# A two-layer decoder trunk on one core: gate paths first, values in six groups, masked compression, an opening in units of one and two k-tiles

## The chip, the core and the metric

The kernel runs on one core of one Trainium2 chip. The metric is the device time of one execution in microseconds, as the median of several runs. Engines are named as in the profile: PE (matrix products), PEld (its weight loads), DVE (VectorE), ACT (ScalarE), POOL (GpSimd), SP (the engine whose queue issues nearly all DMA requests).

## The reference

The input is x, 256 tokens of 1024 features in f32, and a conditioning vector c of 1024. Two layers, each `x = x + gate * mixer(rms_norm(x) * (1 + scale) + shift)`, where shift, scale and gate are three parts of `silu(c) @ w_ada + b_ada` (1024 by 3072 for each layer), and a last rms_norm.

The even mixer projects the 256 normalised tokens to 2968 columns and splits them:

- A: eight query heads of 64, one key and one value head, with rope, a sliding window of 128, and a learned sink for each head in the softmax.
- B: eight query heads in two groups, three branches: compressed keys and values (blocks of 32 with stride 16, through a small MLP with two weight matrices of 2048 by 256), selected blocks, and a window of 512. With 256 tokens all blocks are selected, so the second and third branch are causal attention. A sigmoid gate for each head and branch weighs the three.
- za and zb, 512 columns each: the outputs of A and B are multiplied by their silu before one output projection of 1024 by 1024.

The odd mixer projects to q, k, v, z of 1024 each, with 16 heads; with 256 tokens it is causal attention. Its output is multiplied by silu(z) and goes through an output projection of 1024 by 1024.

## The kernel before, in words

**Products.** A projection splits both operands into a rounded part and a rest (`split`: `whi` by ACT, `wlo` by DVE, in pieces of 512 columns) and makes three products for each k-tile (`mm3`: hi by hi, hi by lo, lo by hi). `hhi` and `hlo` hold the normalised input of a layer in that form, 128 features by 256 tokens for each of eight k-tiles; `ghi` and `glo` hold the gated attention output. Scores, transposes, values and small sums are plain f32 products.

**Order.** No engine instruction is issued where the code stands. `Plan.record` (line 229) notes each with what it depends on, and `Plan.issue` (line 259) issues all in the order of a list of numbers, ORDER (line 36), which was written out ahead. So each engine's own order is that list's, and all DMA requests of SP stand in one queue in that order. A request into a buffer waits in that queue until the buffer is free, with all requests behind it. As every instruction is issued from line 256, the profile shows L256 for nearly all, and tiles tell them apart. Buffers come from small rings (`rot`, line 300): five `raw` tiles of 128x2048 for weights, four `t4` of 128x1024, five `sm` and four `pT` for softmax, and eight banks of PSUM in rings ("pj" three, "s" two, "pt", "o" and "m" one each).

**Opening** (lines 647 to 735). c is transposed and its silu goes into `cz`. x is transposed as it is into `xT`; its root mean squares are spread over partitions by a product with ones (`rb`). Then a loop over eight k-tiles g. `start_prep` loads 256 columns of w_ada for k-tile g (128 of shift, 128 of scale; four requests of 256 KB, one k-tile ahead), sums them over 1024 rows, on DVE for `v` in `ST_ON`, on PE for `p`, makes `hhi[g]` and `hlo[g]` (h by DVE, `hhi` from h by ACT, `hlo` by DVE), and loads row block g of W0 in four requests. `start_mm` makes the products of 1688 columns: the queries, keys and values of B, the keys and values of A, the branch gates, and the first half of A's queries. The other half follows as a projection of its own (`ld_qa`, line 749).

**First layer** (lines 737 to 1036). Rope and transposes; `attn_pair` for two heads and one branch: scores, mask and minimum (DVE), exp (ACT), reciprocal and normalisation (DVE, `sm<-sm,rc`), transposes (PE), copies (ACT, `pT`), values (PE). `b_pair` calls it for two branches of two heads, `a_pair` for two heads, `compress` and `cmp_softmax` make the compressed branch, `cmp_pair` adds its output to `oT` with DVE, `fin_o` copies an output to `oT` with ACT, and `gated` (line 970) makes the products of a gate path, takes tanh, and multiplies with `oT`. `fill` puts jobs between them that sum w_ada for this layer's gate and the next layer's shift and scale (`acc`). Then `out_proj`, in which `add_scaled` adds to x.

**Second layer** (lines 1039 to 1221). Normalisation and transposes, then four times: values, queries and keys of four heads (`split_quad`, `rot_quad`), `attn_quad`, which ends with an ACT copy of 128x512 to `oT`. The four gate paths come behind all attention in the program. The output projection, the last normalisation and the store end it.

Of the kernel before, what the change touches and what calls it, by code (L numbers as in the profile page):

```python
# [7 lines left out]
F32 = mybir.dt.float32  # L8
# [5 lines left out]
P = 128  # L14
# [8 lines left out]
ST_ON = "ppvvpvvp"  # L23
AHEAD = 1
# [4 lines left out]
CUT = 384  # L29
T4B = 4  # L30
# [151 lines left out]
class Plan:  # L182
# [46 lines left out]
    def record(self, eng, name, args, kw):  # L229
# [11 lines left out]
        for a in banks:  # L241
            p0, p1, _ = self._box(a)
            uses.append((a.tensor.name + "#", (p0, p1, 1), eng.key == "pe" and not accum))
# [1049 lines left out]
```

## Time and profile before

| | |
|---|---|
| median of 3 runs | 318.71 us (318.41 to 320.02) |
| profiled execution | 317.62 us |
| its span in the profile | 315.8 us |
| mean granted clock of PE | 0.99 |
| DMA | 71.85 MB, mean 227 GB/s |

The span is the time from the first to the last instruction that the profile shows; 1.8 us of the profiled execution lie around it. A row of a group gives the engine, the operation, the tiles written and read, the shape and the count, then busy us and mean ns of one, then idle time ahead of them. Instructions of one engine overlap a little, so counts times means come out somewhat above busy time. An f32 product shows as two instructions on PE. A busy PE isn't a PE at its peak: ends of products are modelled.

### The profile page before, as it was taken

To read this page: it belongs to the slowest core of one execution; us is meant where nothing else is said; L and a number is where in the kernel's file an instruction comes from. 1 tells how busy PE (TensorE), PEld (TensorE's weight loads), DVE (VectorE), ACT (ScalarE), POOL (GpSimd) and SP (SyncE) were. 2 spreads that over 40 slices of the span, in tenths; PEclk is the share of its full clock that TensorE was granted. 3 is DMA by queue.
4 is the path that set the end of the run, shared out by engine and by line. 5 is a ranking of instruction groups with operands and counts; after the bars stand their busy time and mean duration, and the time that the engine had idled before them with its cause. 6 is when DMAs were issued, how large, how long until landed. Compare 5 with 4: busy or idle time off the path is not lost.

```text
span 315.8 us, 6311 instructions
## 1 busy us (share of the span) xinstructions
PE 300.0 (95%) x2246; PEld 251.0 (79%) x2246; DVE 271.1 (86%) x744; ACT 189.9 (60%) x481; POOL 12.3 (4%) x30
## 2 busy tenths in 40 slices
PE   6788999999899999999999999999999999999991
PEld 6656787887677677898787689997899889988890
DVE  0289998999999999999998967787999998996873
ACT  3445435783758797797356675382965497654611
POOL 4200000000000000000010100000000000000021
PEclk9799999999999999999999999999999999999998
DMA  5999999999989954829699957646188644651003
GB/s 188 315 323 317 332 319 338 324 347 345 345 258 330 290 179 135 260 82 324 196 298 320 327 145 251 206 120 205 49 279 270 203 131 138 211 200 60 1 2 133
DMA packets 71280, 71.85 MB, mean 227 GB/s; under 512 B 3080, under 2 KB 62928, under 8 KB 71248
## 3 DMA queue, kind: packets, MB, share of 16 engines
q1 hardware_dynamic: 70528, 70.90, 72.0%
q10 hardware_dynamic: 592, 0.48, 0.5%
q8 instruction: 18, 0.29, 0.4%
q14 instruction: 14, 0.11, 0.1%
q0 software_dynamic: 128, 0.05, 0.1%
HBM read 70.38 MB, written 1.05 MB: 226 GB/s over the span
## 4 chain that ended last, share of the span: by engine, by line
PE 57%; DVE 22%; DMA 9%; ACT 4%; issue 4%; SPq 2%; POOL 1%; POOLq 0%; ACTq 0%; DVEq 0%
PE ps_pj L256 41%; DVE t L256 5%; DVE acc L256 5%; PE ps_pt L256 5%; PE ps_s L256 5%; PE ps_o L256 5%; DVE wlo L256 4%; DVE sm L256 4%; PE ps_m L256 2%; SPq L256 2%; DMA qT<-in_w_ada_dram 2%; DMA gate<-in_w_ada_dram 2%; DMA snk<-in_a_sinks_dram 2%; DMA raw<-in_w_in_even_dram 2%; DMA raw<-in_w_in_odd_dram 2%
## 5 line engine op out<-in xcount | busy, mean ns | idle before, releaser
L256 ACT CAST whi<-raw 128x512 fp32r<-128x512 f32 (+1 forms) x132 | 76.4, 600 | 47.4 <-PE ps_pj L256 28.9
L256 DVE TENSOR_TENSOR wlo<-raw,whi 128x512 fp32r<-128x512 f32 (+1 forms) x116 | 74.4, 659 | 5.4 <-ACT whi L256 5.3
L256 PE MATMUL ps_pj<-hhi,whi 128*128 128x256 f32 x256 | 73.0, 289 | 0.0
L256 PE MATMUL ps_pj<-hhi,wlo 128*128 128x256 f32 x256 | 72.2, 285 | 0.0
L256 PE MATMUL ps_pj<-hlo,whi 128*128 128x256 f32 x256 | 72.0, 283 | 0.0
L256 PEld LDWEIGHTS ps_pj<-hhi,whi 128*128 128x128 f32 x256 | 47.9, 188 | 1.4 <-issue 0.8
L256 PEld LDWEIGHTS ps_pj<-hlo,whi 128*128 128x128 f32 x256 | 48.1, 188 | 0.7 <-issue 0.3
L256 PEld LDWEIGHTS ps_pj<-hhi,wlo 128*128 128x128 f32 x256 | 47.9, 188 | 0.5 <-issue 0.2
L256 ACT ACTIVATE sm<-sm,mn 128x128 f32<-128x128 f32 (+1 forms) x76 | 34.1, 450 | 12.0 <-DVE mn L256 11.9
L256 DVE SCALAR_TENSOR_TENSOR acc<-raw,cz,acc 128x512 f32<-128x512 f32 x42 | 31.4, 746 | 0.5
L256 PE MATMUL ps_pj<-wlo,hhi 128*128 128x512 f32 (+2 forms) x72 | 27.3, 379 | 0.0
L256 PE MATMUL ps_pj<-whi,hhi 128*128 128x512 f32 (+2 forms) x72 | 26.3, 381 | 0.8 <-ACT hhi L256 0.7
L256 PE MATMUL ps_pj<-whi,glo 128*128 128x512 f32 (+1 forms) x72 | 26.7, 371 | 0.0
L256 PE MATMUL ps_pj<-wlo,ghi 128*128 128x512 f32 (+1 forms) x72 | 26.7, 371 | 0.0
L256 PE MATMUL ps_pj<-whi,ghi 128*128 128x512 f32 (+1 forms) x72 | 26.6, 374 | 0.0
L256 PE MATMUL ps_pj<-whi,hlo 128*128 128x512 f32 (+2 forms) x72 | 26.4, 368 | 0.0
L256 DVE SCALAR_TENSOR_TENSOR wlo<-raw,whi 128x512 fp32r<-128x512 f32 x32 | 21.0, 688 | 3.7 <-ACT whi L256 3.4
L256 DVE TENSOR_SCALAR sm<-sm,rc 128x256 f32<-128x256 f32 (+1 forms) x76 | 21.8, 318 | 0.3
L256 ACT COPY pT<-ps_pt 128x384 f32<-128x384 f32 x33 | 15.5, 471 | 10.2 <-PE ps_pt L256 9.5
L256 PE MATMUL ps_pt<-ta,sm 128*128 128x128 f32 x114 | 20.4, 280 | 0.0
L256 PEld LDWEIGHTS ps_pt<-ta,sm 128*128 128x128 f32 x114 | 13.0, 141 | 4.8 <-issue 2.9
L256 PEld LDWEIGHTS ps_pj<-whi,hhi 128*128 128x128 f32 x72 | 13.3, 188 | 3.6 <-ACT hhi L256 1.4
(206 smaller groups left out, 566.3 us busy)
## 6 DMA issues: line engine op xcount, KB each, us to landing
raw<-in_w_in_odd_dram SPq DMA_DIRECT2D x16, 1024.0 KB, 5.7
raw<-in_w_ada_dram SPq DMA_DIRECT2D x28, 512.0 KB, 5.6
qT<-in_w_ada_dram SPq DMA_DIRECT2D x24, 256.0 KB, 5.8
raw<-in_w_in_even_dram SPq DMA_DIRECT2D x5, 1024.0 KB, 7.2
raw<-in_w_in_even_dram SPq DMA_DIRECT2D x8, 576.0 KB, 5.5
raw<-in_w_out_even_dram SPq DMA_DIRECT2D x4, 1024.0 KB, 5.1
raw<-in_w_out_odd_dram SPq DMA_DIRECT2D x4, 1024.0 KB, 5.4
gate<-in_w_ada_dram SPq DMA_DIRECT2D x8, 256.0 KB, 6.1
```

What stands on the lines that cost most here:

```text
L256: self.ops.append(dict(key=eng.key, deps=deps, fn=lambda: getattr(real, name)(*args, **kw)))
```

## The change

- **Opening.** x is normalised first (two `tensor_scalar` on DVE and two scaled copies on ACT) and then transposed, so `rb` and its product with ones go. `hhi` comes from `xT` by ACT directly, h by a `tensor_scalar`. The conditioning comes in units of 1, 2, 2, 2 and 1 k-tiles (`START`: k-tiles in a unit, and how many of the eight row blocks of w_ada DVE sums); PE sums the rest in products of 128 columns, four at a time, followed by one transpose. The contiguous pieces of w_ada are 256 columns long in a unit of two. A row block of W0 comes in two requests. A's second half of queries is now in it and the first half follows on its own.
- **Small loads.** norm_g and b_ada are asked for by ACT's queue instead of POOL's; the positional rows of the compression have a tile of their own.
- **Twenty products** of ones into a bank ("o") that nobody reads before it is written again. In the new list 17 of them stand behind the first of the twelve warm-up products; the other three and the remaining warm-up products stand between the first transposes.
- **Attention of the first layer.** `attn_four` handles two heads and two branches (B) or four heads (A); the second, 256-wide normalisation of each second head is done by ACT (`ON_ACT`). Values of a group are made at the end in one go (`attn_values`), for B together with those of the compressed branch: two groups for A and four for B. The rings `sm` and `pT` get three more tiles each out of `bigA`.
- **Gates.** `gate_path` comes ahead of the attention that it belongs to and leaves `(1 + tanh) z` in `oT`; `gated` multiplies the attention output in PSUM with it, with no copy between. In the second layer too. The order of the first layer is A, compression, B.
- **Compression.** `kcbd` and `vz` are written by one instruction each, with a mask `blk` that holds 0.5 and 0, instead of two and eight; the two memsets go.
- The rule for dependencies inside a PSUM bank also orders the last product of a sum; some banks of PSUM change rings from the output projection on; the jobs for the second layer's gate are spread over its attention. ORDER is a new list of 3112 numbers in place of 3107.

```diff
-ST_ON = "ppvvpvvp"
-AHEAD = 1
+START = ((1, 0), (2, 4), (2, 6), (2, 6), (1, 4))
+GROUPED = 1
+ON_ACT = ((0, 1, 1), (1, 1, 1))
...
-    G.dma_start(rows[0:16, :], norm_g.rearrange("l (k p) -> (l k) p", p=P))
-    G.dma_start(rows[16:64, :], b_ada.rearrange("l (k p) -> (l k) p", p=P))
+    A.dma_start(rows[0:16, :], norm_g.rearrange("l (k p) -> (l k) p", p=P))
+    A.dma_start(rows[16:64, :], b_ada.rearrange("l (k p) -> (l k) p", p=P))
...
+    keep = bank("o")
+    for _ in range(20):
+        T.matmul(keep[:, :P], ones, ones, start=True, stop=True)
...
+    for t in range(2):
+        r = r0[:, t, :]
+        A.activation(t4(), xs[:, t, :], AF.Square, scale=D**-0.5, accum_out=r[:, 0:1])
+        G.tensor_scalar(r[:, 0:1], r[:, 0:1], EPS, None, op0=ALU.add)
+        G.tensor_tensor(r[:, 1:2], r[:, 0:1], ex0[:, 0:1], ALU.pow)
+        xn = t4()
+        V.tensor_scalar(xn[:, :512], xs[:, t, :512], r[:, 1:2], None, op0=ALU.mult)
+        A.mul(xn[:, 512:], xs[:, t, 512:], r[:, 1:2])
...
+    def start_ada(g, n, room):
+        src = w_ada[0].rearrange("(k p) (s c) -> p k s c", p=P, c=D)
+        kk = 4 // n
+        w = []
+        for i in range(2 * n):
+            wt = room[i].rearrange("p (k s c) -> p k s c", k=kk, s=2)
+            for s in range(2):
+                Y.dma_start(wt[:, :, s, :], src[:, kk * i : kk * i + kk, s, P * g : P * (g + n)])
+            w += [wt[:, k] for k in range(kk)]
+        return w
+    def start_sums(g, n, d, w):
+        a = sb([P, 512], "acc", 1)
+        av = a[:, : 256 * n].rearrange("p (s c) -> p s c", s=2)
+        for k in range(d):
+            if k == 0:
+                V.tensor_scalar(av, w[k], cz[:, k, 0:1], None, op0=ALU.mult)
+            else:
+                V.scalar_tensor_tensor(av, w[k], cz[:, k, 0:1], av, op0=ALU.mult, op1=ALU.add)
...
-        Y.dma_start(raw[:, 1432:1688], W0[g * P : (g + 1) * P, 0:256])
-        Y.dma_start(raw[:, 0:1152], W0[g * P : (g + 1) * P, 1152:2304])
-        Y.dma_start(raw[:, 1152:1280], W0[g * P : (g + 1) * P, 512:640])
-        Y.dma_start(raw[:, 1280:1432], W0[g * P : (g + 1) * P, 2304:2456])
+        Y.dma_start(raw[:, 0:1304], W0[g * P : (g + 1) * P, 1152:2456])
+        Y.dma_start(raw[:, 1304:1688], W0[g * P : (g + 1) * P, 256:640])
...
-        V.scalar_tensor_tensor(h, xT[:, g, :], shs[:, 0, 1, g : g + 1], rb, op0=ALU.mult, op1=ALU.mult)
-        A.activation(hhi[:, g, :], h, AF.Identity, bias=shs[:, 0, 0, g : g + 1])
-        V.scalar_tensor_tensor(hlo[:, g, :], h, shs[:, 0, 0, g : g + 1], hhi[:, g, :].bitcast(F32), op0=ALU.add, op1=ALU.subtract)
+        A.activation(hhi[:, g, :], xT[:, g, :], AF.Identity, bias=sh, scale=sc)
+        V.tensor_scalar(h, xT[:, g, :], sc, sh, op0=ALU.mult, op1=ALU.add)
+        V.tensor_tensor(hlo[:, g, :], h, hhi[:, g, :].bitcast(F32), ALU.subtract)
...
+                for t, (a, b) in enumerate(((0, P), (P, 3 * P))):
+                    if (n, i, t) in ON_ACT:
+                        A.mul(sms[i][:, a:b], sms[i][:, a:b], rc[:, n, i, t : t + 1])
+                    else:
+                        V.tensor_scalar(sms[i][:, a:b], sms[i][:, a:b], rc[:, n, i, t : t + 1], None, op0=ALU.mult)
...
+        V.tensor_tensor(
+            vz,
+            pv[:, : 2 * HD].rearrange("p (g d) -> p g d", g=2).unsqueeze(2).to_broadcast([P, 2, 4, HD]),
+            blk[:, 0:4].unsqueeze(1).unsqueeze(3).to_broadcast([P, 2, 4, HD]),
+            ALU.mult,
+        )
...
+    def gate_path(w, zc, ft, tag="pj"):
         pz = proj_F(w, zc, tag)
+        th = oT[:, ft : ft + 2, :].rearrange("p j s -> p (j s)")
         A.activation(th, pz, AF.Tanh, scale=0.5)
         V.scalar_tensor_tensor(th, th, 1.0, pz, op0=ALU.add, op1=ALU.mult)
+    def gated(po, ft, n, coef):
+        V.scalar_tensor_tensor(oT[:, ft : ft + n, :], po[:, : n * S].rearrange("p (a s) -> p a s", s=S), coef, oT[:, ft : ft + n, :], op0=ALU.mult, op1=ALU.mult)
+    def gated_parts(ft):
+        A.copy(ghi[:, ft : ft + 2, :], oT[:, ft : ft + 2, :])
+        V.tensor_tensor(glo[:, ft : ft + 2, :], oT[:, ft : ft + 2, :], ghi[:, ft : ft + 2, :].bitcast(F32), ALU.subtract)
...
+    fill(1)
+    gate_path(W0, 640, 0)
+    a_quad(0)
+    gate_path(W0, 640 + 256, 2)
+    a_quad(1)
     compress()
     cmp_softmax()
+    fill(1)
+    gate_path(W0, 2456, 4)
+    b_pair(0, True)
...
-        A.copy(oT[:, 2 * u : 2 * u + 2, :], po.rearrange("p (a s) -> p a s", a=2))
+        gated(po, 2 * u, 2, 0.5)
+        gated_parts(2 * u)
+    jobs += ada_jobs(ada_gate, 1, G1_ON, 2)
...
+        gate_path(W1, 3 * D + 256 * u, 2 * u, "p1")
         attn_quad(u, qk)
-    jobs += ada_jobs(ada_gate, 1, G1_ON, 2)
-    fill()
-    for u in range(4):
-        gated(W1, 3 * D + 256 * u, 2 * u, 0.5, "p1")
         fill()
```

More of the change, by code (lines that the diff above doesn't have):

```diff
@@ L242, in record @@
             p0, p1, _ = self._box(a)
-            uses.append((a.tensor.name + "#", (p0, p1, 1), eng.key == "pe" and not accum))
+            uses.append((a.tensor.name + "#", (p0, p1, 1), eng.key == "pe" and (not accum or bool(kw.get("stop")))))
         for nm, b, w in uses:
@@ new lines, in attn_four, with attn_values @@
+        return pts
+    def attn_values(po, jobs):
+        ids = []
+        for n, (cs, keys) in enumerate(jobs):
+            for m, (os, heads) in enumerate(keys):
+                for i in range(2):
+                    ids.append(T.matmul(
+                        po[64 * i : 64 * i + 64, cs + os.start : cs + os.stop],
+                        heads[i][0],
+                        heads[i][1],
+                        start=n == 0 and m == 0,
+                        stop=n == len(jobs) - 1 and m == len(keys) - 1,
+                        skip_group_check=True,
+                        tile_position=(0, 64 * i),
+                    ))
+        plan.group(ids)
@@ L647, in tile_trunk, with keys_of @@
+    def keys_of(vcols, pts):
+        return [
+            (os, [(vcols(b), pts[i][:, ks]) for i in range(2)])
+            for b, (ks, os) in enumerate(((slice(0, S), slice(0, S)), (slice(S, 3 * P), slice(P, S))))
+        ]
     bigA = const([P, 2304], "bigA")
@@ L679, in tile_trunk @@
     acc = [[bank("s"), bank("pj"), bank("pj")], [bank("s"), bank("pj"), bank("o")]]
-    acc_qa = bank("pt")
+    acc_w = bank("pt")
     spare = [sb([P, 4, S], "qT", 3).rearrange("p k f -> p (k f)") for _ in range(3)] + [gate]
-    spare = (spare[0:2], spare[2:4])
-    acc0 = sb([P, 512], "acc", 1)
-    halves = {}
-    def start_prep(g):
-        for j in range(g, min(KT, g + AHEAD + 1)):
-            if j not in halves:
-                halves[j] = ada_tile(0, (j, 8 + j), spare[j % 2])
-        w = halves[g]
-        if ST_ON[g] == "v":
-            a = acc0[:, (g % 2) * 256 : (g % 2) * 256 + 256]
-            V.tensor_scalar(a, w[0][:, 0, :], cz[:, 0, 0:1], None, op0=ALU.mult)
-            for k in range(1, KT):
-                V.scalar_tensor_tensor(a, w[k // 4][:, k % 4, :], cz[:, k, 0:1], a, op0=ALU.mult, op1=ALU.add)
-            ada_shift_scale(0, g, 1, a=a, st=ones)
-        else:
-            ada_shift_scale(0, g, 1, a=ada_rows(w))
+    more = [t4() for _ in range(T4B)]
@@ L729, in start_mm @@
             )
-    prep = start_prep(0)
-    for g in range(KT):
-        nxt = start_prep(g + 1) if g + 1 < KT else None
-        start_mm(g, *prep)
-        prep = nxt
+    rooms = [spare[0:2], more, spare, more, spare[0:2]]
+    ahead, g = start_ada(0, START[0][0], rooms[0]), 0
+    for u, (n, d) in enumerate(START):
+        w, rows_w = ahead, [start_row(g)]
+        if u + 1 < len(START):
+            ahead = start_ada(g + n, START[u + 1][0], rooms[u + 1])
+        rows_w += [start_row(g + v) for v in range(1, n)]
+        start_sums(g, n, d, w)
+        preps = [start_prep(g + v, rows_w[v]) for v in range(n)]
+        for v in range(n):
+            start_mm(g + v, *preps[v])
+        g += n
     Y.dma_start(tb, tbl_b[:, :1056])
@@ L955, in cmp_pair @@
-    def cmp_pair(hp_):
-        g = hp_ // 2
-        po = bank("o")
-        for i in range(2):
-            T.matmul(
-                po[64 * i : 64 * i + 64, :S],
-                vz[:, g, (2 * hp_ + i) % 4, :],
-                pcT[:, g, :],
-                start=True,
-                stop=True,
-                tile_position=(0, 64 * i),
-            )
-        V.tensor_tensor(oT[:, 4 + hp_, :], oT[:, 4 + hp_, :], po[:, :S], ALU.add)
-    def gated(w, zc, ft, coef, tag="pj"):
+    for n, (tag, bufs) in enumerate((("sm", SMB), ("pT", 4))):
+        sb([P, 3 * P], tag, bufs)
+        ring[tag][0] += [bigA[:, 3 * P * m : 3 * P * m + 3 * P] for m in range(3 * n, 3 * n + 3)]
@@ new lines, in tile_trunk, with a_quad, keys @@
+    pj_banks, s_banks = ring["ps_pj"][0], ring["ps_s"][0]
+    ring["ps_pj"] = [pj_banks[0:3], 0]
+    m_banks = ring["ps_m"][0]
+    ring["ps_s"] = [s_banks + pj_banks[3:3], 0]
+    def a_quad(u):
+        def keys(i):
+            rs = slice(64 * i, 64 * i + 64)
+            return lambda n, t: (qaT[rs, 2 * u + n, t * P : (t + 1) * P], kTb[rs, 4, : P * (t + 1)])
+        sk = [[[snk[:, o + 4 * u + 2 * n + i : o + 4 * u + 2 * n + i + 1] for i in range(2)] for n in range(2)] for o in (8, 0)]
+        pts = attn_four([keys(0), keys(1)], maska, sk, None)
+        po = bank("o")
+        attn_values(po, [(n * S, keys_of(lambda b: vb[:, b, 2, :], pts[n])) for n in range(2)])
+        gated(po, 2 * u, 2, 0.5)
+        gated_parts(2 * u)
@@ L1028, in out_proj @@
             fill()
-            py = proj_T(ld, ghi, glo, n == 1)
+            py = proj_T(ld, ghi, glo, n == 1, "po")
             fill()
```

340 lines of the change are left out of this document (164 added, 176 removed), and 262 rows, old and new, of the table ORDER.

## The prediction

> **What bounds the kernel now.** I read the page first, then the busy times by stretch, then the request queue, then the groups of instructions. Of the page:
>
> ```profile
> span 315.8 us, 6311 instructions
> PE 300.0 (95%) x2246; PEld 251.0 (79%) x2246; DVE 271.1 (86%) x744; ACT 189.9 (60%) x481; POOL 12.3 (4%) x30
> PE 57%; DVE 22%; DMA 9%; ACT 4%; issue 4%; SPq 2%; POOL 1%; POOLq 0%; ACTq 0%; DVEq 0%
> ```
>
> Three engines are near full on average, so the stage has to be asked. Busy time by stretch; the columns are the stretch, its length, then busy us and instructions of PE, PEld, DVE, ACT, POOL, then granted clock, DMA share and GB/s:
>
> ```profile
> 8.00:16.00 8.00, 6.50 (x46) 5.06 (x50) 1.95 (x10) 3.92 (x9) 1.71 (x4) 0.79 1.16 316
> 16.00:62.00 46.00, 43.69 (x255) 33.83 (x248) 41.13 (x99) 22.45 (x51) 0.00 (x0) 1.00 1.10 324
> 62.00:70.00 8.00, 8.00 (x56) 7.09 (x56) 7.91 (x19) 7.19 (x20) 0.00 (x0) 1.00 1.10 355
> 70.00:80.00 10.00, 9.86 (x106) 7.65 (x109) 9.70 (x43) 4.32 (x16) 1.58 (x3) 1.00 1.09 343
> 62.00:146.00 84.00, 82.08 (x722) 65.57 (x722) 83.23 (x303) 62.84 (x196) 1.58 (x3) 1.00 0.82 264
> 146.00:180.00 34.00, 33.80 (x187) 25.51 (x186) 31.72 (x67) 19.38 (x39) 2.56 (x4) 1.00 0.93 285
> 180.00:283.00 103.00, 103.00 (x875) 93.75 (x874) 90.31 (x229) 65.88 (x160) 0.00 (x0) 1.00 0.60 189
> 283.00:303.00 20.00, 20.00 (x101) 16.77 (x100) 15.62 (x24) 10.72 (x20) 0.90 (x2) 1.00 0.08 27
> ```
>
> To 62 us (the opening, the eight k-tiles of the first projection) the DMA engines are full at 316 to 324 GB/s. From 62 to 146 (ropes, compression, the six attention pairs of each kind, gate paths) DVE is busy 83.23 of 84 us: it is the bound. From 180 on PE is busy without a gap and DVE has 12.7 us to spare in 103, so there DVE relief buys nothing. The chain of waits says the same: DVE in a row at 96 us, PE from 180 to the end (start, length, what):
>
> ```profile
> 96.42 0.46 DVE sm L256 x2
> 161.37 1.80 DVE wlo L256 x3
> 180.10 22.39 PE ps_pj L256 x159
> 283.06 20.20 PE ps_pj L256 x99
> ```
>
> **The opening.** Per k-tile it asks for 1 MB of conditioning weights (four requests of 256 KB, a quarter of them into the tile gate, the others in the first row below) and 844 KB of W0 in four requests, 1.91 MB in all. The requests, and two of the row batches in the queue's own order of time:
>
> ```profile
> qT<-in_w_ada_dram SPq DMA_DIRECT2D x24, 256.0 KB, 5.8
> raw<-in_w_in_even_dram SPq DMA_DIRECT2D x8, 576.0 KB, 5.5
> raw<-in_w_in_even_dram SPq DMA_DIRECT2D x8, 128.0 KB, 4.8
> raw<-in_w_in_even_dram SPq DMA_DIRECT2D x8, 76.0 KB, 5.0
> raw<-in_w_in_even_dram SPq DMA_DIRECT2D x8, 64.0 KB, 5.2
> 23.11 2.26 SPq L256 DMA_DIRECT2D raw<-in_w_in_even_dram  x4
> 35.03 2.26 SPq L256 DMA_DIRECT2D raw<-in_w_in_even_dram  x4
> ```
>
> From 23.11 to 35.03 two k-tiles pass: 5.96 us each, which is 1.91 MB at 321 GB/s. The queue issues a row batch in 2.26 us, so it isn't the bound; the bytes are. The change moves the same bytes. But its conditioning weights come for two k-tiles at once, so each contiguous piece is 256 columns (1 KB) instead of 128 (512 B) in six of eight k-tiles, and a row of W0 comes in two pieces instead of four. The nearest row for 1 KB pieces is 62 to 80 us, where gate columns and compression weights come at 355 and 343 GB/s. At 349, a k-tile takes 5.48 us; six of them save 6 x 0.48 = 2.9 us, and the two whose rows alone improve perhaps half of that each: 3.4. The first row of W0 is now asked for behind four conditioning requests instead of eight; that starts PE earlier but not the end of the stream, and I give it and the two saved requests 0.7 us. **Opening: -4.1 us.** Bounds: 0 if the rate stays and nothing else matters; -7 if all eight k-tiles came at 355 (5.39 us each, -4.6) and the earlier start counted for a k-tile's wait of 2.4 more.
>
> The Trainium skill (DMA: Bandwidth & Descriptors, Specifications) says that pieces of 512 B and more already move at line rate. By that rule the 3.4 us would be zero and the opening would gain only the 0.7; the rows above (321 against 349) speak against it without proving it, since the stretches differ in more than the size of piece.
>
> DVE must keep up with this. Mean ns of one in the third number after the count:
>
> ```profile
> L256 DVE SCALAR_TENSOR_TENSOR oT<-bigA,shs,oT 128x256 f32<-128x256 f32 x8 | 3.9, 484 | 0.2
> L256 DVE SCALAR_TENSOR_TENSOR hlo<-oT,shs,hhi 128x256 fp32r<-128x256 f32 x8 | 3.9, 482 | 0.7 <-ACT hhi L256 0.6
> L256 DVE TENSOR_TENSOR hlo<-t,hhi 128x256 fp32r<-128x256 f32 x8 | 3.4, 422 | 2.4 <-ACT hhi L256 2.3
> L256 DVE TENSOR_SCALAR acc<-qT,cz 128x256 f32<-128x256 f32 x4 | 1.4, 346 | 0.0
> L256 DVE SCALAR_TENSOR_TENSOR acc<-qT,cz,acc 128x256 f32<-128x256 f32 x20 | 9.7, 484 | 0.6
> L256 DVE SCALAR_TENSOR_TENSOR acc<-raw,cz,acc 128x512 f32<-128x512 f32 x42 | 31.4, 746 | 0.5
> L256 DVE TENSOR_SCALAR t<-xs,parts 128x512 f32<-128x512 f32 x2 | 1.0, 488 | 0.8 <-POOL parts L256 0.8
> ```
>
> h becomes a tensor_scalar (484 to about 346 ns, eight times: 1.1 us), hlo a plain subtraction (482 to 422: 0.5). The sums of the conditioning go from 4 x 0.346 + 28 x 0.484 = 14.9 us to 3 x 0.49 + 13 x 0.746 + 0.346 + 3 x 0.484 = 13.0 us. Normalising x first adds two tensor_scalars of 0.49 and two copies out of PSUM of about 0.6: 2.2. Net -1.3 us of 41.13: DVE stays near full once the opening is 4.1 us shorter, which is why I don't take the -7.
>
> **The twenty products** nobody reads: by the written order 17 stand right behind the first warm-up product, three later among the transposes. PE now (the rows below) has 24 half-products of ones in 5.05 us, 0.21 each, and then nothing until x and the identity arrive at 8.74:
>
> ```profile
> 1.06 5.05 PE L256 MATMUL ps_m<-ones 128*128 128x128 f32 x24 [1.06 <-DVE ones L256]
> 8.74 0.51 PE L256 MATMUL ps_s<-ta,xs 128*128 128x128 f32 x2 [2.63 <-DMA ta<-in_tbl_a_dram]
> 6.19 1.06 ACT L256 ACTIVATE t<-xs 128x1024 f32<-128x1024 f32 x1 [2.52 <-DMA xs<-in_x_dram]
> 17.88 0.74 PE L256 MATMUL ps_pj<-whi,hhi 128*128 128x512 f32 x2
> ```
>
> Eighteen products are 36 halves, 7.6 us, so they end at 8.6: the wait for x hides them. The clock, 0.79 in the stretch after the idle time, should stay up. Cost 0, because the first real product at 17.88 waits for the DMA and the conditioning, not for PE; from -1 (faster transposes) to +4 if that cover fails (rival 4). The requests for norm_g and b_ada move from POOL's queue to ACT's, ahead of the squares of x; ACT stood idle for 2.52 us before these (row at 6.19), which hides two issues. The masks are written on POOL in that time too.
>
> **The middle.** DVE is the bound, so I count what leaves it. The rows:
>
> ```profile
> L256 DVE TENSOR_SCALAR sm<-sm,rc 128x256 f32<-128x256 f32 x38 | 13.2, 356 | 0.2
> L256 DVE TENSOR_TENSOR oT<-oT,ps_o 128x256 f32<-128x256 f32 x4 | 1.7, 414 | 0.0
> L256 DVE TENSOR_SCALAR vz<-ps_m 32x64 f32<-32x64 f32 x8 | 1.8, 220 | 0.1
> L256 DVE SCALAR_TENSOR_TENSOR t<-oT,t 128x512 f32<-128x512 f32 x8 | 5.5, 686 | 0.2
> L256 DVE TENSOR_TENSOR t<-ps_pj,tb 128x512 f32<-128x512 f32 x16 | 10.4, 683 | 0.2 <-PE ps_pj L256 0.2
> L256 ACT ACTIVATE sm<-sm,mn 128x256 f32<-128x256 f32 x38 | 19.1, 503 | 4.9 <-DVE mn L256 4.9
> L256 ACT COPY oT<-ps_o 128x256 f32<-128x256 f32 x9 | 3.3, 370 | 1.2 <-PE ps_o L256 1.0
> ```
>
> Twelve 256-wide normalisations go to ACT (two of eight in each of six attention calls): 12 x 0.356 = 4.3 us; two in a row take less than their sum (0.46 at 96.42 against 0.28 + 0.36), so 12 x 0.27 = 3.2 is the lower bound. The four additions of the compressed branch go, since its products now accumulate in the same bank: 4 x 0.414 = 1.7 (1.3 in a row). Eight small vz writes (1.8) become one 128x512 one (0.68 by the nearest PSUM row), kcbd's two become one: -1.2. The last gate multiplication of the B heads becomes four of 256 (0.484 each) for two of 512 (0.686): +0.6. Sum -6.6, in a row -5.1. ACT gets twelve scaled copies (0.37 to 0.50 each, 4.4 to 6.0 us) and loses eight copies of 0.37 (3.0): +1.4 to +3.0 on 62.84 of 84, which its idle time hides; uncovered, it would cost that. One step is moved past others: the compression's 4 MB are now asked for behind two gate columns of 1 MB (5.7 us at 349), and its first 16 products stand in PE's queue ahead of the first scores, behind which DVE's mask passes wait. The ropes, on DVE before these, cover it; without them it costs those 5.7. **Middle: -5.0 us**, the lower sum, because PE is also busy 82.08 of 84 and becomes the bound soon after. Bounds: +0.7 if the 5.7 comes on top, 0 if ACT or PE takes the place, -8 if the new order (gate products first, as work for PE while the softmax chains run) also fills PE's waits.
>
> **The second layer.** PE's products are the same; the gate of each four heads is now multiplied straight out of PSUM and four 128x512 copies leave ACT, which is no bound. What gets worse is the end: the last work is now the attention of heads 12 to 15, no longer a gate path. After its scores DVE has, by the written order, eight mask passes (about 0.28 to 0.42 each, 2.8), eight normalisations (2.5), two reciprocals (0.3) and seven 512-wide instructions of other kinds (0.69 each, 4.8): 10.4 us to the last normalisation. PE has in that time 38 gate products at 0.141 (22.39 us for 159 in the chain), 10 of the output projection at 0.204 (20.20 for 99), 12 transposes and eight value products (about 2.7): 10.1 us. Then gated, ghi and glo, 2.0 us, over 8 products of 0.204. Shortfall 0.3 + 0.4. **Second layer: +0.5 us**, from -0.5 to +3.
>
> **Sum:** -4.1 - 5.0 + 0.5 = -8.6. The profiled execution took 317.62 us (span 315.8 and 1.8 around it), so 309.0; the median of the runs, 318.71, is 1.1 above it, so **310.1 us**.
>
> **Rivals.** (1) **The opening keeps its rate**: the rule above. Then -0.7 - 5.0 + 0.5 = -5.2: 313.5 us. For it, the DMA share of 1.10 is the same at 324 and at 355 GB/s. (2) **All of it adds up**: -7 - 8 = -15: 303.7. For it, PE waits in the middle only because DVE is late; against it, PE is close behind. (3) **ACT takes DVE's place** in the middle: its instructions run in order, and exponentials queue behind scaled copies that wait for a reciprocal. The middle's 5.0 is gone, -4.1 + 0.5: 315.1, give or take 3. (4) **The products don't hold the clock** and stand ahead of the transposes: 32 products and 16 transposes at half clock are 64 x 0.21 + 16 x 0.21 = 16.8 us, so the first real product comes at 22 instead of 17.88, and DVE's 41 us of opening end at 63: +1 - 5.0 + 0.5, 315.2, give or take 2. (5) **Slower: the end of the second layer is exposed.** If the gate products of the last four heads have run out before its scores are there, the chain of 10.4 + 2.0 us stands uncovered: -9.1 + 12.4 = +3.3, 322.0. It decides from 10.7 us of uncovered chain. Against it, the written order keeps 38 of those 48 products behind the scores; for it, DVE is 88% busy there and every lateness of it lengthens the chain.
>
> **How the numbers follow.** Forecast 0.50 (305 to 313), rival 1 0.16, rival 2 0.10, rival 3 0.10, rival 4 0.04, rival 5 0.10. About 0.5% (1.6 us) can be told from no change. Faster by more: 0.50 + 0.16 + 0.10 and two thirds of rivals 3 and 4: 0.83; within: 0.07, the rest of 3 and 4 and the near edge of 5; slower: 0.10. The range from 303 to 317.5 leaves out rival 5, the lower half of rival 2 and the upper edge of 3 and 4, some 0.18.
>
> **What would show it.** Right: the opening moves 340 GB/s or more and PE leaves the eighth k-tile near 57 us; DVE still near full in the middle with some 5 us less work; the second layer from its first projection to the last product as long as now within a microsecond. Wrong: a rate of 320 in the opening; ACT above 90% in the middle with DVE waiting for it; a PE wait of microseconds ahead of the last value products; a clock below 1 after 8 us.

## The result, and the profile after

The changed kernel takes 309.35 us against 319.26 us: a ratio of 0.968 (95% interval 0.963 to 0.972). A second set of five rounds gave 308.49 against 319.49, ratio 0.966 (0.963 to 0.969). The forecast was 310.1 us, between 303 and 317.5, so it was right in size. Its sum of parts has to be read apart from that: the two large stages came out near their sizes, and their reasons held only in part. (One execution of the first set, with a granted clock of 0.752 from start to end, took 365.21 us: the ratio leaves it out, the median does not and is 309.12 without it, and the medians below hold the few long executions too, which moves none of them by more than 0.3 us.) The profile below is of the second set, from an execution of 307.29 us.

From the page of the changed kernel, the span, the engines and the shares of the chain:

```profile
span 305.5 us, 6393 instructions
PE 294.8 (97%) x2332; PEld 252.3 (83%) x2332; DVE 261.8 (86%) x709; ACT 191.3 (63%) x484; POOL 11.4 (4%) x35
PE 87%; DVE 4%; DMA 4%; ACT 2%; issue 1%; POOL 1%; POOLq 0%; SPq 0%; DVEq 0%
```

DVE had 22% of the chain before and has 4% now; PE went from 57% to 87%. Busy time by stretch, in the columns of the prediction's table (stretch, length, busy us of PE, PEld, DVE, ACT, POOL, granted clock, DMA share, GB/s):

```profile
8.00:16.00 8.00, 7.00 (x77) 5.65 (x76) 5.20 (x16) 4.76 (x11) 0.46 (x1) 1.00 1.04 349
16.00:62.00 46.00, 44.70 (x323) 37.32 (x324) 40.81 (x89) 25.51 (x65) 0.00 (x0) 1.00 1.07 369
62.00:146.00 84.00, 83.81 (x737) 68.58 (x736) 82.65 (x291) 66.18 (x196) 1.58 (x3) 1.00 0.84 271
180.00:283.00 103.00, 103.00 (x877) 94.01 (x876) 86.58 (x222) 61.27 (x147) 0.00 (x0) 1.00 0.56 179
```

From 16 to 62 us the transfers run at 369 GB/s where they ran at 324. From 62 to 146 both PE (83.81 of 84) and DVE (82.65) are near full; PE's 1.92 us of gaps there are down to 0.19. The clock column has no 0.79 any more in these stretches.

Three events that both kernels have cut the span into stages: DVE's first rope instruction ends the opening, PE's first product of the second layer's projection ends the first layer, PE's last product ends the second. Start, length and what, first of the kernel before, then of the changed one:

```profile
60.05 1.23 DVE L256 TENSOR_TENSOR t<-t,tb 128x224 f32<-128x224 f32 x3 [0.69 <-ACT t L256]
173.99 0.50 PE L256 MATMUL ps_pj<-whi,hhi 128*128 128x512 f32 x1
308.65 0.27 PE L256 MATMUL ps_pj<-whi,glo 128*128 128x256 f32 x1
```

```profile
55.28 1.23 DVE L258 TENSOR_TENSOR t<-t,tb 128x224 f32<-128x224 f32 x3 [0.72 <-ACT t L258]
164.37 0.50 PE L258 MATMUL ps_pj<-whi,hhi 128*128 128x512 f32 x1
298.41 0.27 PE L258 MATMUL ps_pj<-whi,glo 128*128 128x256 f32 x1
```

| stage | before | after | difference | predicted |
|---|---|---|---|---|
| opening | 60.05 | 55.28 | -4.8 | -4.1 |
| first layer behind it | 113.94 | 109.09 | -4.9 | -5.0 |
| second layer | 134.66 | 134.04 | -0.6 | +0.5 |

The sum is -10.2 us in one execution of each; the medians differ by 9.9 and 11.0. The opening varies between executions: in three traces of runs below that leave it alone it ends at 55.91, 56.28 and 56.65, and in a run of the kernel before that leaves it alone at 60.30, so its difference is some 3.4 to 5 us. Stage by stage the table looks like the forecast. The experiments ask whether it came about in the way that the forecast said.

### The profile page after: what moved, and what is told of

Same layout as the page of the kernel before. It is cut to its first block, busy times and chain, and to the rows that moved or that the text cites. A ratio compares the mean times of both kernels' runs of the same rounds, so it can differ in the third digit from the quotient of the medians.

```text
span 363.4 us, 6393 instructions
## 1 busy us (share of the span) xinstructions
PE 353.9 (97%) x2332; PEld 289.9 (80%) x2332; DVE 265.9 (73%) x709; ACT 193.0 (53%) x484; POOL 11.4 (3%) x35
## 4 chain that ended last, share of the span: by engine, by line
PE 93%; DMA 2%; ACT 1%; DVE 1%; issue 1%; POOL 0%; POOLq 0%; SPq 0%; DVEq 0%
PE ps_pj L258 54%; PE ps_s L258 13%; PE ps_o L258 9%; PE ps_m L258 8%; PE ps_pt L258 8%; DMA raw<-in_w_in_even_dram 2%; ACT whi L258 1%; DVE t L258 1%; POOL parts L258 0%; DVE xs L258 0%; ACT t L258 0%; POOLq L1360 0%; SPq L258 0%; ACT kTb L258 0%; ACT hhi L258 0%
## 5 line engine op out<-in xcount | busy, mean ns | idle before, releaser
L258 PE MATMUL ps_pj<-hhi,whi 128*128 128x256 f32 x256 | 81.5, 324 | 0.0
L258 PE MATMUL ps_pj<-hlo,whi 128*128 128x256 f32 x256 | 81.5, 322 | 0.0
L258 PE MATMUL ps_pj<-hhi,wlo 128*128 128x256 f32 x256 | 80.8, 321 | 0.0
L258 PEld LDWEIGHTS ps_pj<-hlo,whi 128*128 128x128 f32 x256 | 54.8, 215 | 1.3 <-issue 0.8
L258 PEld LDWEIGHTS ps_pj<-hhi,wlo 128*128 128x128 f32 x256 | 54.5, 214 | 1.2 <-issue 0.6
L258 PEld LDWEIGHTS ps_pj<-hhi,whi 128*128 128x128 f32 x256 | 54.4, 214 | 0.8 <-issue 0.3
L258 PE MATMUL ps_pj<-whi,hlo 128*128 128x512 f32 (+2 forms) x72 | 30.3, 421 | 0.0
L258 ACT ACTIVATE sm<-sm,mn 128x256 f32<-128x256 f32 (+1 forms) x58 | 25.9, 448 | 7.7 <-DVE mn L258 7.4
L258 PEld LDWEIGHTS ps_pj<-whi,hlo 128*128 128x128 f32 x72 | 14.5, 201 | 3.5
L258 PEld LDWEIGHTS ps_pj<-wlo,hhi 128*128 128x128 f32 x72 | 14.5, 202 | 3.3 <-issue 0.2
```

Of the source, the lines that this page charges most:

```text
L258: self.ops.append(dict(key=eng.key, deps=deps, fn=lambda: getattr(real, name)(*args, **kw)))
```

## The experiments

Differences are between medians, each against the kernel that the edit starts from: 308.49 us for the changed kernel, the runs beside it for the kernel before. The interval of that 308.49 is about 1 us to either side, so less than 1 us is not told from nothing. The runs were made in three sets, on different chips; the kernel before has 319.49, 319.68 and 319.27 in them.

### The changed kernel again

> The changed kernel as it is, for a profile at the full granted clock, read stage by stage against the profile of before. Forecast's terms: opening -4.1 us, middle -5.0, second layer +0.5, in all -8.6, so a ratio near 0.973. Right: the opening moves 340 GB/s or more, DVE's work in the first layer falls by about 5 us, and the second layer keeps its length within 1 us. Rival 1 (the opening keeps its rate) would show 320 GB/s and an opening shorter by under 1 us; then the 10 us measured must come from the middle. Rival 2 would show 7 and 8 us.

Measured: 308.49 us, span 305.5; the profile above is this run's.

### The opening: the size of the pieces, or the number of requests

Two kernels cut each of the 24 conditioning requests of the two-tile units in two, one by columns (512 B pieces), one by rows (1 KB pieces); both then have 48 of 128 KB.

```
-  Y.dma_start(wt[:, :, s, :], src[:, kk*i : kk*i+kk, s, P*g : P*(g+n)])
+  for j in range(2):                          # by columns
+      Y.dma_start(wt[:, :, s, j*P : j*P+P], src[:, kk*i : kk*i+kk, s, P*(g+j) : P*(g+j+1)])
or
+  for j in range(2):                          # by rows
+      Y.dma_start(wt[:, j, s, :], src[:, kk*i+j, s, P*g : P*(g+n)])
```

> The changed kernel, with each of the 24 conditioning requests of the two-tile units cut into two requests by columns: the same bytes in pieces of 512 B, two requests of 128 KB each. Theory (1 KB pieces move faster, the forecast's opening term): six k-tiles lose up to 0.48 us each, so 2 to 3 us slower than the run that cuts them by rows. Rival 1 (512 B is enough for line rate): the same as the run cut by rows, within 0.5 us.

> As the run with 512 B pieces, but each request is cut by rows of the weight matrix: again two requests of 128 KB, in pieces of 1 KB. It prices the number of requests alone. Theory: 24 more issues of about 0.5 us in a queue that has some 2.5 us to spare for each k-tile cost nothing, within 0.5 us of the changed kernel. If the queue is the bound after all, both cut runs are 5 us or more slower.

Measured: 318.67 us by columns and 316.59 by rows. The size of the piece was worth 2.1 to 2.4 us between them, as expected, but 24 more requests at the same size of piece cost some 8 us (7.8 to 8.1), which the theory there had put at nothing. So either the number of requests had been the bound all along, or the cut had made a new one. Two further kernels separate these. The first brings 512 B pieces in the old number of requests (the first layer's conditioning then reads half of its columns from elsewhere in the matrix; the amount of work is the same):

```
+  four = w_ada[0].rearrange("(k p) (m c) -> p k m c", p=P, c=4*P)
+  Y.dma_start(wt[:, s, :, :].rearrange("p s (j c) -> p (s j) c", c=P),
+              four[:, kk*i + s, 0:4, P*(g%4) : P*(g%4) + P])
```

> The changed kernel with the 24 conditioning requests of its two-tile units fetched in pieces of 512 B instead of 1 KB, in the same number of requests of the same 256 KB (half of the columns of the first layer's shift and scale then come from elsewhere in the matrix, so the values differ and the work doesn't). If the size of the piece sets the rate, as the prediction had it: the DMA engines stay full, at about 320 to 330 GB/s in place of 350 to 397, and the time rises by 3 to 5 us. If the number of requests in SP's queue was all (the rival that the first runs left): within 1 us of the changed kernel, with an unchanged rate.

The second takes requests off SP's queue in the kernel before:

```
-  Y.dma_start(raw[:, 1432:1688], W0[g*P : (g+1)*P, 0:256])
+  G.dma_start(raw[:, 1432:1688], W0[g*P : (g+1)*P, 0:256])
   Y.dma_start(raw[:, 0:1152], W0[g*P : (g+1)*P, 1152:2304])
   ...                          # the other two small ones likewise
```

> The kernel before with the three small requests of each W0 row (128, 76 and 64 KB; 24 requests in all) issued by POOL's queue instead of SP's; the same bytes in the same pieces. If the bytes and the size of their pieces bound the opening, as the prediction had it (the queue issues a row batch in 2.26 us, so it isn't the bound), the time stays within 1 us of the kernel before. If the number of requests that one queue issues one after the other bounds it (24 further requests cost the changed kernel 8.1 us), moving 24 of 64 away makes it 4 to 8 us faster. If every request costs the DMA engines time wherever it is issued, the time stays too, but then the small requests in the trace still land late.

Measured: the 512 B pieces take 311.95 us, 3.5 more than the changed kernel (3.0 more than 308.93, which a run that leaves the opening alone took in the same set); the small row requests on POOL's queue take 323.33 against 319.68, 3.6 more than the kernel before, where the expectation had the same or less. The stretch from 16 to 56 us of five kernels, in this order: before, changed, 512 B in the same requests, 1 KB in twice the requests, before with POOL's queue. The last two columns are the DMA share and GB/s:

```profile
16.00:56.00 40.00, 37.69 (x223) 28.45 (x216) 35.87 (x88) 18.09 (x40) 0.00 (x0) 1.00 1.11 325
```

```profile
16.00:56.00 40.00, 38.70 (x287) 32.04 (x288) 34.81 (x77) 20.02 (x48) 0.00 (x0) 1.00 1.07 371
```

```profile
16.00:56.00 40.00, 36.49 (x265) 29.76 (x266) 31.68 (x70) 16.62 (x38) 0.00 (x0) 0.96 1.07 343
```

```profile
16.00:56.00 40.00, 33.65 (x228) 26.72 (x228) 29.66 (x64) 14.42 (x33) 0.00 (x0) 0.96 0.95 308
```

```profile
16.00:56.00 40.00, 35.32 (x186) 26.78 (x179) 33.04 (x80) 15.19 (x33) 7.98 (x15) 0.91 1.09 325
```

Read the share beside the rate. With 1.07 to 1.11 the transfer engines are full, and the rate is what their pieces allow: 325 GB/s before, 343 with the conditioning in 512 B, 371 with it in 1 KB. The difference between the first two comes from the end of the stretch alone: in the 8 us from 16, 24 and 32 us on, the rates are 321, 319 and 331 before, 325, 318 and 329 with 512 B, and 357, 385 and 397 in the changed kernel, so the rows in two pieces brought nothing that shows while the conditioning ran. The packet records of the traces say the same without any rate: between 16 and 56 us a packet of 512 B takes a transfer engine 31 ns on average in the kernel before and 29 in the one with 512 B, and a packet of 1 KB 49 ns in the changed one, where two of 512 B would take 58 to 62.

Taking 24 of 64 requests off the queue leaves 325, so the queue was not the bound before. With the requests cut the share is 0.95 at 308: the engines are no longer full, and the queue is the bound. It shows in its own rows, of the changed kernel and of the one cut by rows (t is the tile that half of the two-tile requests fill):

```profile
24.94 7.42 SPq L258 DMA_DIRECT2D t<-in_w_ada_dram  x8
L258 SPq DMA_DIRECT2D t<-in_w_ada_dram x8: 367/368/955, 24.9 to 31.4; - x8
SPq L258 <- DMA raw<-in_w_in_even_dram: 2.4, 2, 1.2
```

```profile
30.49 11.52 SPq L261 DMA_DIRECT2D t<-in_w_ada_dram  x16
L261 SPq DMA_DIRECT2D t<-in_w_ada_dram x16: 327/372/1059, 30.5 to 41.6; - x16
SPq L261 <- DMA raw<-in_w_in_even_dram: 2.9, 3, 1.5
```

The second row of each has the shortest, median and longest issue in ns: a request takes SP some 0.37 us whether it asks for 256 or for 128 KB. The issues alone add up to 3.6 of the 7.42 us in which eight of 256 KB pass (2 MiB, 283 GB/s), and to 7.0 of the 11.52 us of sixteen of 128 KB (the same bytes, 182 GB/s). So 3.5 of the 4.1 us more are time of issuing. The third row is a wait for an earlier request of another tile, raw, to land; with those for other tiles such waits are 3.7 us in the first stretch and 2.9 in the second, so they didn't grow. Over the whole opening, 24 more issues of 0.37 us are 8.9 us of the queue's time, close to the 8 us measured: in the kernel cut by rows, 50 of the 60 issues between 10 and 50 us follow the one ahead within 0.15 us.

The changed kernel stands close to a second limit of its queue. At no issue of the opening, in the traces of the kernel before, the changed one, the one with 512 B and the one cut by rows, were more than seven earlier requests of the queue seen unlanded, and in the changed kernel 20 of the 44 issues between 10 and 50 us come within 0.1 us of the landing of the eighth before (in the one cut by rows, 9 of 60). The traces show why: the queue's requests report their landing on eight semaphores in turn, so a request waits for the one that used its semaphore last. That is how these programs are built, and no run shows a limit of the chip there. That the wait costs anything while the engines are full is not shown either. So the 8 us are the price of crossing from a bound by pieces to one by the queue, not one that the kernel before paid.

That POOL's queue made the kernel before slower, at the same 325 GB/s, is read from its chain: the row batch that PE needs lands later. Start, length and what, of the kernel before and of the one with POOL's queue:

```profile
23.99 5.50 DMA raw<-in_w_in_even_dram
```

```profile
25.01 7.86 DMA raw<-in_w_in_even_dram
```

With its own queue the small requests of later rows start ahead of bytes that are needed sooner. That this is all of the 3.6 us is not shown.

### The twenty products

```
-    for _ in range(20):
+    for _ in range(0):
         T.matmul(keep[:, :P], ones, ones, start=True, stop=True)
```

> The changed kernel without the twenty products that nobody reads. Forecast: they cost nothing and bring nothing that the path sees, because the opening waits for bytes: the same time within 1 us, with the granted clock at half for some 3 us after the warm-up. Rival: they hold the clock for the transposes and the first conditioning sums, and without them the first weight product comes 1 to 2 us later; then the kernel is slower by that if PE or DVE, not the bytes, sets the end of the opening. Rival 4 (they stand in the way) would make this run faster.

Measured: 310.73 us, 2.2 more than the changed kernel (ratios 0.972, interval 0.970 to 0.974, against 0.966). Start, length and what on PE, first with the products, then without, there with a window and the end of the opening:

```profile
8.08 0.83 PE L258 MATMUL ps_m<-ones 128*128 128x128 f32 x6
15.88 0.38 PE L258 MATMUL ps_pt<-whi,hhi 128*128 128x256 f32 x1 [0.77 <-ACT hhi L258]
```

```profile
8.35 1.49 PE L259 MATMUL ps_m<-ones 128*128 128x128 f32 x6
17.60 0.39 PE L259 MATMUL ps_pt<-whi,hhi 128*128 128x256 f32 x1 [1.18 <-ACT hhi L259]
26.00:28.00 2.00, 1.45 (x5) 1.34 (x6) 2.00 (x6) 0.99 (x3) 0.00 (x0) 0.61 1.07 353
59.12 1.23 DVE L259 TENSOR_TENSOR t<-t,tb 128x224 f32<-128x224 f32 x3 [0.73 <-ACT t L259]
```

Without them the same six half-products of ones take 1.49 us instead of 0.83, and the first real product comes 1.7 us later. The Trainium skill (TensorE: Matmul & The Clock Gate, What's actually happening) says that an idle array falls back to half rate and that some microseconds of work release it; 1.49 to 0.83 is a factor of 1.8, which fits. The clock column doesn't show this slow start: it prints 1.00 from 8 to 16 us of this run, and the trace's clock records begin only at 12.8 us (at 4.7 in the changed kernel), so the slow rate is read from the lengths alone. The window shows the clock at 0.61 at 26 us, after PE had waited 1.48 and 0.86 us.

The last row matters most. Without the products the opening ends at 59.12 us, only 0.9 sooner than in the kernel before, although the pieces of 1 KB are there and the transfers run at 351 GB/s from 16 to 56 us. With the products and 512 B it ends at 59.27:

```profile
59.27 1.23 DVE L259 TENSOR_TENSOR t<-t,tb 128x224 f32<-128x224 f32 x3 [0.72 <-ACT t L259]
```

So in these traces the gain of the opening needs both steps; either alone, with the rest of the change, leaves less than 1 us of it.

Eight products of the same kind were then put into the kernel before:

```
     T.matmul(ring_warm[:, :P], ones, ones, start=True, stop=True)
+    for _ in range(8):
+        T.matmul(ring_warm[:, :P], ones, ones, start=True, stop=True)
```

> The kernel before with eight further unread products of ones behind its last one, in the idle time ahead of x; nothing else differs. The prediction gave unread products no price here, since the first real product waits for the transfers and the conditioning: within 1 us. In the changed kernel, whose opening is bound by PE's start, taking away twenty of them cost 2.2 us. If holding the clock is worth that much by itself, the granted clock of the stretch from 8 to 16 us rises from 0.79 to 1.00 and the time falls by 1 to 2 us here too; if the transfers, full at 320 GB/s, set the opening of this kernel, the clock rises and the time stays.

Measured: 318.84 against 319.27, ratio 0.999 (0.997 to 1.001): no difference. A row of PE in the kernel before, then two rows and a stretch of the one with eight more:

```profile
9.04 0.85 PE L256 MATMUL ps_pj<-ta,xs 128*128 128x128 f32 x3
```

```profile
9.09 0.49 PE L258 MATMUL ps_pj<-ta,xs 128*128 128x128 f32 x3
17.76 0.89 PE L258 MATMUL ps_pj<-whi,hhi 128*128 128x512 f32 x2 [0.66 <-ACT whi L258]
16.00:24.00 8.00, 6.71 (x29) 5.38 (x28) 6.09 (x16) 2.86 (x6) 0.00 (x0) 0.79 1.13 320
```

The transposes of x ran at full clock (0.49 us for three instead of 0.85), and the first real product still came at 17.76 instead of 17.88, because it waits 0.66 us for the cast of a row that arrives when it arrives. That the eight products did this is not shown: in the trace of the kernel before with normalisations on ACT (below), which has the same opening and no further products, three transposes take 0.49 us too, and the first real product also starts at 17.76. In both the clock falls later instead, at the first real products (0.79 from 16 to 24 us here, 0.57 there, where the kernel before has 1.00). What both show is that the cover that the prediction named does exist in the kernel before: transposes that end more than 1 us sooner don't move the first real product. The change had moved the first row forward, and there PE's start was among the last things to be ready.

One kernel tried to bring that start forward by order alone: four products of ones moved behind the first conditioning sums, and the first shift of the gate ahead of the casts on ACT.

```
 # written order, PE:   ... ones x4, conditioning sums, ...
 #                  ->  ... conditioning sums, ones x4, ...
 # written order, ACT:  ... casts of row 0, copy of the sums, ...
 #                  ->  ... copy of the sums, casts of row 0, ...
```

> The changed kernel with four of the products of ones moved from ahead of the first conditioning sums to behind them, and the first shift of the gate ahead of row 0's casts on ACT; all else, the number of products too, is the same. In the changed kernel the coefficients of the first conditioning sum are ready at 11.26 us and the sums start at 12.50 us. If the start of the first projection sets the end of the opening (PE is unbroken from 29 us on), the time falls by 0.5 to 1.5 us. If DVE or the transfers set it, it stays within 0.5 us. If the clock needs the products at that place, it gets up to 2 us slower.

Measured: 308.67 us, no difference. The sums do come earlier, at 11.59 instead of 12.50, but the shift doesn't (rows of the reordered kernel):

```profile
11.59 1.08 PE L259 MATMUL ps_m<-qT,cz 128*32 128x128 f32 x32
13.55 1.43 DVE L259 TENSOR_TENSOR wlo<-raw,whi 128x512 fp32r<-128x512 f32 x2 [1.16 <-ACT whi L259]
14.90 0.15 DVE L259 TENSOR_REDUCE asb<-ps_m 128x2 f32<-128x4 f32 x1
```

The reduction that yields the shift stands behind two subtractions (1.43 us together) in DVE's order and comes at 14.90 (14.65 in the changed kernel). The time gained in one queue was lost to the order of the next, so this run doesn't tell what an earlier start would be worth.

### The middle: the twelve normalisations

Given back to DVE, and doubled on ACT:

```
-ON_ACT = ((0, 1, 1), (1, 1, 1))
+ON_ACT = ()
or
+ON_ACT = ((0, 0, 1), (0, 1, 1), (1, 0, 1), (1, 1, 1))
```

> The changed kernel with its twelve normalisations of the first layer (two of eight 256-wide ones in each of six attention calls) given back from ACT to DVE; nothing else differs. Theory of the prediction: DVE bounds the middle (82.6 of 84 us busy from 62 to 146 in the changed kernel), so the time rises by 12 x 0.27 to 12 x 0.356 us, 3.2 to 4.3 us, to about 312 us. Rival 3 (ACT takes DVE's place): the time stays within 1 us or falls. A third account, formed after the first runs: PE is nearly full from 29 us on and the changed kernel is set by PE's total, so DVE's extra work partly falls into what PE has in store: 1 to 3 us.

> The changed kernel with twice as many 256-wide normalisations of the first layer's attention on ACT (24 in place of 12). Theory of the prediction, carried on: DVE loses another 3.2 to 4.3 us in its bound stage and ACT still has idle time, so 3 us less. Rival 3: ACT, in whose queue exponentials then stand behind twice as many scaled copies, becomes the end of the softmax chain: no gain, or a loss of 1 to 3 us. The account by PE's total: PE is busy 97% of the span, so the gain is under 1 us.

Measured: 310.97 us with all on DVE, 2.5 more than the changed kernel (ratio 0.972, 0.970 to 0.975), where the prediction's theory had 3.2 to 4.3; 308.63 with 24 on ACT, no difference, where it had 3 less. Busy time from 62 to 146 us, first with all on DVE, with that run's two boundaries, then with 24 on ACT:

```profile
62.00:146.00 84.00, 82.19 (x711) 67.17 (x710) 82.64 (x299) 59.06 (x180) 1.58 (x3) 1.00 0.81 259
55.91 1.23 DVE L258 TENSOR_TENSOR t<-t,tb 128x224 f32<-128x224 f32 x3 [0.73 <-ACT t L258]
168.31 0.50 PE L258 MATMUL ps_pj<-whi,hhi 128*128 128x512 f32 x1
```

```profile
62.00:146.00 84.00, 83.85 (x739) 68.65 (x739) 80.38 (x281) 70.17 (x210) 1.58 (x3) 1.00 0.85 271
```

Without the move the stage takes 112.40 us instead of 109.09, 3.3 more, and PE has 1.81 us of gaps again instead of 0.19. With twice the move DVE falls to 80.38 and PE stays at 83.85 of 84: nothing is left to gain. The gaps tell only half of it, 1.6 of the 3.3 us. The rest lies inside PE's busy time, 110.59 us of the stage against 108.90 for 887 and 886 products. A product of the stage takes 0.33 us on average and the next starts after 0.12, so a short wait hides behind the product that is still running and doesn't show as a gap.

The same step alone in the kernel before:

```
-  V.tensor_scalar(pp[:, a:b], pp[:, a:b], rc[:, i, t : t+1], None, op0=ALU.mult)
+  (A.mul(pp[:, a:b], pp[:, a:b], rc[:, i, t : t+1]) if i and t
+   else V.tensor_scalar(pp[:, a:b], pp[:, a:b], rc[:, i, t : t+1], None, op0=ALU.mult))
```

> The kernel before with the twelve 256-wide normalisations of the first layer's attention on ACT instead of DVE; nothing else differs. Theory of the prediction: DVE, busy 83.23 of 84 us in the middle, loses 3.2 to 4.3 us, so 3 to 4 us faster, about 316. The account by PE (in the changed kernel the same step was worth 2 to 2.5 us, because PE became full): here PE has 1.9 us of waits in the same 84 us, so at most about 2 us faster. Rival 3 (ACT takes DVE's place): no gain.

Measured: 318.65 against 319.27, ratio 0.998 (0.996 to 1.000): 0.6 us, not the 3 to 4 that follow from the prediction. Two stretches of the kernel before, and then three rows of the edited one: a stretch, the one in which ACT is full, and the wait there (engine, what it waited for, us, times, longest):

```profile
100.00:120.00 20.00, 19.95 (x179) 14.88 (x178) 20.00 (x85) 16.89 (x58) 0.00 (x0) 1.00 0.71 228
120.00:147.00 27.00, 27.00 (x231) 23.16 (x231) 26.93 (x82) 21.12 (x64) 0.00 (x0) 1.00 0.60 197
```

```profile
62.00:146.00 84.00, 81.70 (x719) 64.94 (x718) 80.65 (x292) 66.61 (x207) 1.57 (x3) 1.00 0.81 261
110.00:120.00 10.00, 9.03 (x83) 6.96 (x83) 8.40 (x42) 9.62 (x33) 0.00 (x0) 1.00 0.49 154
PE ps_pt L256 <- ACT pT L256: 1.0, 1, 1.0
```

DVE lost 2.6 us of work (83.23 to 80.65) and PE gained none (82.08 to 81.70). From 100 us on PE had been full in the kernel before, 19.95 of 20 and 27.00 of 27, side by side with DVE; and from 110 to 120 ACT is now busy 9.62 of 10 and PE waits 1.0 us for it, which is what rival 3 described. Which of the two took the gain, PE's own work or ACT, isn't told apart.

### The second layer

Eight normalisations there from DVE to ACT:

```
-  V.tensor_scalar(sms[j][:, a:b], sms[j][:, a:b], rc[:, j, t : t+1], None, op0=ALU.mult)
+  (A.mul(...) if j % 2 and t else V.tensor_scalar(...))      # same operands
```

> The changed kernel with eight 256-wide normalisations of the second layer's attention moved from DVE to ACT. Theory of the prediction: from 180 us on PE is busy without a gap and DVE relief buys nothing: within 0.5 us. Rival: if the end of the second layer hangs on the chain of the last heads, in which DVE works in a row (10.4 us by the prediction), the last normalisations leaving it make it 0.5 to 1 us faster; if ACT's queue delays that chain, 0.5 to 1 us slower.

Measured: 308.93 us, 0.4 more and inside the uncertainty. Over the whole span DVE's busy time fell from 261.8 to 260.6 us. In the changed kernel and in this one, from 180 to 280:

```profile
180.00:280.00 100.00, 100.00 (x864) 91.58 (x863) 84.98 (x220) 60.86 (x146) 0.00 (x0) 1.00 0.57 182
```

```profile
180.00:280.00 100.00, 100.00 (x864) 92.08 (x862) 84.94 (x213) 64.14 (x157) 0.00 (x0) 1.00 0.56 179
```

PE has no gap in either, and the relief of DVE bought nothing there.

## Why the prediction was right or wrong

**The opening (-4.1; measured -4.8): right in size, its mechanism right for the transfers and incomplete for the rest.** "The queue issues a row batch in 2.26 us, so it isn't the bound; the bytes are": moving 24 requests away left 325 GB/s. The size of the piece matters as said: a packet of 1 KB takes 49 ns and two of 512 B 58 to 62, and undoing the 1 KB pieces of the conditioning costs 3.0 to 3.5 us. The rate was mis-sized: 349 forecast, 369 reached, because the nearest row (355 at 62 to 80 us) was no ceiling. The part of the 3.4 us for rows in two pieces, and the 0.7 for the earlier first row and the two saved requests, were not shown. By the rule of the Trainium skill that rival 1 stood on (DMA: Bandwidth & Descriptors, Specifications: line rate from 512 B on) the size of these pieces would have been worth nothing; here 512 B against 1 KB, in requests of the same number and bytes, is 343 against 371 GB/s, so the measurement decides against it for this case. But the transfers alone don't make the 4.1: without the twenty products, which had no part in this term, the opening was 0.9 us shorter than before. That the size came out is in part luck. The text also missed how near the queue's own limit lay: 24 requests more were past it.

**The twenty products (0; measured -2.2): wrong.** The step that failed is "Cost 0, because the first real product at 17.88 waits for the DMA and the conditioning, not for PE". That was true of the trace of before, where transposes that ended sooner changed nothing. It was carried over to a kernel in which the same change asks for the first row earlier; there the transposes and the conditioning sums on PE were among the last links, and at the slow rate the first real product comes 1.7 us later. The gain even lay outside the bounds that were given (-1 to +4). A wait that hides a cost has to be looked up in the trace as the other parts of the change leave it.

**The middle (-5.0; measured -4.9): right in size, wrong in cause.** The failed step is "From 62 to 146 ... DVE is busy 83.23 of 84 us: it is the bound". PE stood at 82.08 in the row beside it and was full from 100 us on. Two engines were near full at once, and relief of one was worth what the others could still take: alone in the kernel before, the normalisations gave 0.6 us of the 3.2 to 4.3. In the changed kernel the same move is worth 2.3 to 2.5 by the medians (310.97 against 308.63 and 308.67 in its own set, 308.49 in the first) and 3.3 by the stage. So the price came near only together with the rest of the change; that the new order, with gate products first, did this, which the prediction had counted only as an upside (rival 2), is likely and not shown. The rest of the stage's gain, 113.94 to 112.40, some 1.5 us, belongs to the additions, the mask and the order together, and was not taken apart. Nor do PE's gaps account for the stage: they fell by 1.7 us, and PE's busy time by another 3.1 (112.03 to 108.90, for 890 and 886 products). ACT was priced at +1.4 to +3.0 and rose from 62.84 to 66.18, 3.3.

**The second layer (+0.5; measured -0.6): just outside its bounds (-0.5 to +3), and the other way.** Of the shortfall of 0.7 us at the end nothing shows in the length. Rival 5 didn't come, and DVE relief there is worth nothing, as said. In the traces of the runs that leave it alone the second layer takes 133.95 to 134.44 us in the changed kernel and 134.66 to 136.46 in the kernel before, so if anything it became shorter; why was not asked.

**The sum.** -8.6 was forecast and -9.9 measured. Undone one by one, the pieces cost 3.0 to 3.5, the products 2.2 and the normalisations 2.3 to 2.5, but these can't be added up: the first two share the opening, and each needs the other. Rival 1 fell (the rate rose), rival 3 in the changed kernel (ACT stayed at 66 of 84 us; in the kernel before it came in part), rival 4 too (the clock held at 1.00 from 8 to 283 us). Of rival 2 the part came true that PE's waits in the middle would be filled, 1.7 us. The chance given for "faster by more" is a slip: its own parts, 0.50, 0.16, 0.10 and two thirds of 0.14, add up to 0.85 and not 0.83.

## What to carry to other kernels

Where two engines are both near full in a stage, a step that relieves one is worth what the others can still take, so ask that before counting DVE's microseconds. PE's gaps are a first answer and too small a one, because its products overlap and hide short waits. A cost hidden behind a wait is hidden only as long as that wait stays; when the same change shortens the wait, price it again. Two steps that open the same stage can be worth little one by one and much together, so undo each alone and look where the stage ends. Read the transfer share beside the rate: in this opening, full engines meant that the size of the pieces set the rate, and engines that weren't full meant that the queue did.

## What the runs showed of the hardware

Pieces of 512 B and of 1 KB, in requests of the same number and bytes, differ: 343 and 371 GB/s from 16 to 56 us with the engines full both times, and a packet of 1 KB takes 49 ns where two of 512 B take 58 to 62. SP's queue took some 0.37 us for a request of 256 KB and of 128 KB alike, so 24 more requests cost some 8 us. It never had more than eight in flight, which the eight semaphores of these programs explain. Requests moved to POOL's queue add no bandwidth while the engines are full (325 GB/s both ways). Waits of PE of 1.48 and 0.86 us were followed by a granted clock below 1 in the opening (0.61 from 26 to 28 us), and where it falls is not the same from one execution to the next: kernels with the same opening show 0.79 from 8 to 16 us and 1.00 behind it, or 1.00 and then 0.57. Twenty unread products were worth 2.2 us in one kernel, and eight more nothing in the other.
